# Recurrence scores in compact 32-token blocks, and one shared ring for three work tiles of the feed-forward stages

## The chip, the cores and the metric

The kernel runs on 1 core of one Trainium2 chip. The metric is device time in microseconds (us) of one execution; several executions are timed and their median is given. The engines are named as in the profile: PE (TensorE, matmuls) with PEld (its weight loads), DVE (VectorE), ACT (ScalarE), POOL (GpSimd), and SP, which here only issues DMAs.

## The reference, cut to what matters

One encoder layer on 256 tokens of 2048 features: SwiGLU feed-forward, a mixing stage with two gated recurrences, cross-attention on 256 memory tokens, a second SwiGLU feed-forward, and RMS norms between them, all in float32. The two parts that the change touches are these.

```python
def swiglu(h, w_up, w_down):                     # twice: d_ff is 5632
    gate, up = jnp.split(h @ w_up, 2, axis=-1)
    return (jax.nn.silu(gate) * up) @ w_down

# HGRN2 recurrence, 8 heads of 128 keys and 128 values, in its chunked form
b = jnp.cumsum(gc, axis=2)                       # gc: log of the forget gate
rel = b[:, :, :, None, :] - b[:, :, None, :, :]
decay = jnp.where(tri[None, None, :, :, None], jnp.exp(jnp.minimum(rel, 0.0)), 0.0)
scores = jnp.einsum('bhtk,bhsk,bhtsk->bhts', qc, kc, decay)
o_intra = jnp.einsum('bhts,bhsv->bhtv', scores, vc)
```

So a score of token t against an earlier token s is a product over 128 keys, each damped by the forget gates between s and t.

## The kernel before, in words

**Operands.** Float32 products are made from split operands: a weight tile `raw` (128x2048) is copied by ACT to a rounded high part `h` (line 120), and DVE subtracts it to leave the low part `l` (line 121). Each product then runs as high by high, high by low and low by high matmuls.

**Order of the work.** `plan` (line 127) lists every weight tile in the order of use. `weights()` (line 165) keeps two tiles ahead: before the matmuls of an entry are written down, the tiles of the next entry are loaded and split. The framework orders each engine's queue from this program order and from its own estimate of the times, and places tiles in the buffers of their pools; the engines execute their queues in order. `raw`, `h` and `l` have 3 buffers each.

**Feed-forward (lines 465 to 568).** The up-projection goes in 11 groups of 512 hidden columns. A group is 8 entries; some are "fast" (7 products in place of 8, at the price of sums of weights formed first), the others "mixed" or "plain". From the fourth group (g = 3) on, the fast entries come in the pairs 1 and 3, 4 and 2, 5 and 7, with a mixed entry between pairs; the second and third group (g = 1, 2) have four fast entries, of which 3 and 5 follow each other. Between groups stand 2 or 4 "down" entries. A fast entry uses, besides `raw`, `h` and `l`, two more tiles of 128x2048:

- `td` (line 211): sums of weights, written by DVE in three steps (lines 213, 214, 215), read by the split into `th` and `tl`;
- `tl` (line 219): the low parts of those sums, written by DVE in two halves (line 121) and read by the last matmuls of the entry (line 452).

A third tile, `ev` (line 525), collects a group's results at its end (lines 533 to 546); PE transposes it (line 489) some entries later, in `turn`. Each of the three has a pool of its own with one buffer.

**Recurrence (`hgrn`, lines 749 to 840).** It runs once for heads 0 to 3 and once for heads 4 to 7 (hf = 0, 1), as a generator that is advanced between the weight tiles of other products: `pump(2)` (line 670) after each unit takes two steps, or fewer where a step yields True. What it issues on an engine is queued behind the last matmul of the product. The 256 tokens are two groups (g) of 128. The scores S of 4 heads and 2 groups, 8 squares of 128 by 128, are built in levels: first the diagonal (lines 757 to 764), then for n = 1, 2, 4, ..., 64 the scores between neighbouring runs of n tokens, with q and k damped between levels (line 800).

- Diagonal: per group, 4 matmuls of 128 by 128 (line 760); DVE multiplies the bank by the identity into S (line 762).
- n below 32: 8 matmuls (line 787), each of a whole group's 128 key tokens against the 64 query tokens of that group that stand in odd runs. DVE multiplies the 128x512 bank by a 0/1 mask into a tile `part` (line 790) and adds that into strided columns of S (line 795). Most of what these matmuls compute is masked away, as only runs that are neighbours count.
- n = 32 and 64: small matmuls that compute only the wanted rectangles (line 777), with 32 or 64 stationary columns. For n = 32 the results go to the bank partitions 0 to 31 and 64 to 95, for n = 64 to 0 to 63. ACT copies them into S (line 780).

After the levels one more block (line 809) gives the scores across the two groups, and lines 819 and 820 apply S to the values.

In the profile a float32 matmul of this part shows as two instructions, each with a weight load of its own.

Of the kernel before, what the change touches and what calls it, by code (L numbers as in the profile page):

```python
# [8 lines left out]
F32 = mybir.dt.float32  # L9
# [4 lines left out]
P = 128  # L14
# [15 lines left out]
for _name, _n in [  # L30
    ("ffn1_norm", 16), ("mix_norm", 16), ("xattn_norm", 16), ("mem_norm", 16),
    ("ffn2_norm", 16), ("hgrn_norm", 8), ("lb0", 8), ("lb1", 8), ("lam", 8), ("conv_w", 32),
    ("conv_b", 8), ("ba", 8), ("bx", 8),
    ("ident", P), ("masks", 64 * 5),
]:
    VEC[_name] = (_at, _n)
    _at += _n
# [24 lines left out]
def block_kernel(ctx: ExitStack, tc: tile.TileContext, xT, xin, memT, vec, gfin, bgate, lruw, wu1, wd1, win, wv,  # L62
# [30 lines left out]
    def bank(name="acc"):  # L93
        return psum.tile([P, 512], F32, name=name, tag="acc")
# [100 lines left out]
    def prepare(src, kind, cuts=1):  # L195

        if kind == "added":
            raw, l = begun.pop(0)
            h = hp.tile([P, 2048], F32R, name="h", tag="h")
            done["high"] = act.activation(h, raw, ACT.Copy).ins  # L200
            return h, l
        raw = rawp.tile([P, 2048], F32, name="raw", tag="raw")
        n = 2048 // cuts
        if kind == "plain":
            h, l = split_tiles()
            for a in range(0, 2048, n):
                sp.dma_start(raw[:, a:a + n], src[:, a:a + n])
                split(h[:, a:a + n], l[:, a:a + n], raw[:, a:a + n])
            return h, l
        sp.dma_start(raw, src)  # L210
        td = scoped["td"].tile([P, 2048], F32, name="td", tag="td")
        two = [v[:, a:a + 1024].rearrange("p (i n) -> p i n", i=2) for v, a in ((td, 0), (raw, 512))]
        dve.tensor_tensor(out=two[0], in0=raw[:, None, :512].broadcast_to([P, 2, 512]), in1=two[1], op=ALU.subtract)  # L213
        dve.tensor_tensor(out=td[:, 1024:1536], in0=raw[:, 1024:1536], in1=td[:, :512], op=ALU.subtract)
        dve.tensor_tensor(out=td[:, 1536:], in0=raw[:, 1536:], in1=td[:, 1024:1536], op=ALU.subtract)
        h, l = split_tiles()
        split(h[:, 512:], l[:, 512:], raw[:, 512:])
        th = hp.tile([P, 2048], F32R, name="h", tag="h")
        tl = scoped["tl"].tile([P, 2048], F32R, name="tl", tag="tl")
        for a in (0, 1024):  # L220
            split(th[:, a:a + 1024], tl[:, a:a + 1024], td[:, a:a + 1024])
        return (h, l), (th, tl)
# [114 lines left out]
            return r  # L337


    FFN_POOLS = dict(td=1, tl=1, ev=1, hd=1)  # L340

    class TokenSquares:

# [121 lines left out]
    def ffn(name, pairs, sq, then, begin=(), sums=(), rstds=()):  # L465
# [39 lines left out]
        for at, e in enumerate(order):  # L505
# [3 lines left out]
            if kind != "down":  # L509
                g, p = e[1:]  # L510
                fast = kind == "fast"
                products = []
                for i, (a, b, n) in enumerate(PRODUCTS[kind]):
                    u = uses[g, n]
                    if u[0] == (p, i):
                        accs[n] = bank()
                    own, less = pairs[p]
                    products.append((accs[n], part(own, a, P) if a >= 0 else part(less, -1 - a, P), part(w[b // 4] if fast else w, b % 4, 512),
                                     u[0] == (p, i), u[-1] == (p, i)))
                three(products)  # L520
                last = at + 1 == len(order) or order[at + 1][1] != g or following == "down"
                ends = kind != "plain" and uses[g, 0][-1][0] == p
                if ends or last:
                    if ends or kind == "plain":
                        ev = scoped["ev"].tile([P, 2048], F32, name="ev", tag="ev")
                        e0, e1, e2, e3 = (ev[:, i * 512:(i + 1) * 512] for i in range(4))
                        if rstds:
                            rstd = rstds[0]
                        if rstd is None:
                            with tc.issue_after(done["high"]):  # L530
                                rstd = sq.rstd_tokens()
                if ends:
                    act.activation(e0, accs[0], ACT.Copy)
                    dve.tensor_tensor(out=e1, in0=accs[5], in1=e0, op=ALU.add)
                    dve.tensor_tensor(out=e2, in0=accs[4], in1=e1, op=ALU.add)
                if last:
                    if kind == "plain":
                        activate(e0, accs[0], accs[1], 0)
                        activate(e3, accs[3], accs[2], 1)
                    else:  # L540
                        for o, n, x in ((e0, 1, e0), (e1, 3, e1), (e1, 2, e1)):
                            dve.tensor_tensor(out=o, in0=accs[n], in1=x, op=ALU.add)
                        activate(e0, e0, e1, 0)
                        for o, n, x in ((e3, 6, e2), (e2, 3, e2)):
                            dve.tensor_tensor(out=o, in0=accs[n], in1=x, op=ALU.add)
                        activate(e3, e3, e2, 1)
                    late.append((4 if g else 2, lambda g=g, hid=(e0, e3): turn(g, hid)))
            else:
                first, n, c, block = e[1:]
                if block == first:  # L550
                    accs["down"] = [bank(), bank()]
                for t in range(2):
                    products = []
                    for k in range(4):
                        a = hids[2 * block + k // 2][:, k % 2 * 512:][:, :512]
                        products.append((accs["down"][t], (a[:, t * P:][:, :P], a[:, T + t * P:][:, :P]),
                                         part(w, k, 512), block == first and k == 0, block == first + n - 1 and k == 3))
                    three(products)
                    if block == first + n - 1:
                        o = xt[c][:, t * 512:(t + 1) * 512]  # L560
                        done["residual"] = dve.scalar_tensor_tensor(out=o, in0=accs["down"][t], scalar=0.5, in1=o,
                                                                    op0=ALU.mult, op1=ALU.add).ins
                        if block == NG - 1:
                            then(c, t)
# [184 lines left out]
    def hgrn(hf):  # L749
# [4 lines left out]
        S = scoped["scores"].tile([P, 3 * 512], F32, name="S", tag="S")  # L754
        Sv = S.rearrange("p (g h t) -> p g h t", g=3, h=4)
        qv, kv = heads(q), heads(kk)
        for g in range(2):
            acc = bank()
            for h in range(4):
                pe.matmul(acc[:, h * P:(h + 1) * P], kv[:, h, g * P:(g + 1) * P], qv[:, h, g * P:(g + 1) * P],  # L760
                          start=True, stop=True)
            dve.tensor_tensor(out=Sv[:, g], in0=acc.rearrange("p (h t) -> p h t", h=4),
                              in1=ident[:, None, :].broadcast_to([P, 4, P]), op=ALU.mult)
            yield
        dve.tensor_tensor(out=q, in0=q, in1=f, op=ALU.mult)
        yield True
        tots = slot(name="tots")
# [1 line left out]
        for li, n in enumerate(LEVELS):  # L769
            acc = bank()  # L770
            if n >= 32:
# [8 lines left out]
                    act.activation(S[a:a + n, :1024].rearrange("p (i t) -> p i t", t=P)[:, :, a + n:a + 2 * n],  # L780
                                   acc[a:a + n, :8 * n].rearrange("p (i n) -> p i n", n=n), ACT.Copy)
                yield
            for g in range(2 if n < 32 else 0):
                for h in range(4):
                    i = g * 4 + h
                    r = qv[:, h, g * P:(g + 1) * P].rearrange("p (j two n) -> p j two n", two=2, n=n)[:, :, 1]
                    pe.matmul(acc[:, i * 64:(i + 1) * 64], kv[:, h, g * P:(g + 1) * P], r, start=True, stop=True)  # L787
            if n < 32:
                part = scoped["tmp2"].tile([P, 512], F32, name="part", tag="part")
                dve.tensor_tensor(out=part.rearrange("p (i t) -> p i t", i=8),  # L790
                                  in0=acc.rearrange("p (i t) -> p i t", i=8),
                                  in1=col("masks", li * 64, 64)[:, None, :].broadcast_to([P, 8, 64]), op=ALU.mult)
                yield
                to = S[:, :1024].rearrange("p (i two n) -> p i two n", two=2, n=n)[:, :, 1]
                dve.tensor_tensor(out=to, in0=to, in1=part.rearrange("p (i n) -> p i n", n=n), op=ALU.add)
                yield
            pairs = tot.rearrange("p (j two) -> p j two", two=2)
            for t, side_of, by in ((q, 1, 0), (kk, 0, 1)):
                o = t.rearrange("p (j two n) -> p j two n", two=2, n=n)[:, :, side_of]
# [291 lines left out]
def _layout(inputs):  # L1091
# [43 lines left out]
    put("bx", vector(a["lru_bx"][0]))  # L1135
    put("lam", vector(a["lru_lambda"][0]))
    put("ident", np.eye(P, dtype=np.float32))
    s, t = np.arange(P)[:, None], np.arange(64)[None, :]
    put("masks", np.concatenate([(s // n == 2 * (t // n)) for n in LEVELS[:5]], axis=1).astype(np.float32))

    w = a["w_in"][0]
    win = columns(np.concatenate([w[:, :2048], w[:, 3072:6144]], axis=1))
# [38 lines left out]
```

## Time and profile before

| What | Value |
|---|---|
| Median of 3 runs | 2468.04 us (2466.79 to 2468.06) |
| Span of the profiled execution | 2467.3 us, 0.7 us below the median of the runs; the profile gives no other time for that execution |
| Instructions | 29103 |
| Mean granted PE clock | 0.998 |
| HBM read, written | 472.17 MB, 2.10 MB |

The profile's page gives busy time per engine; other views give groups of instructions by line, the waits by who released them, the busy time in stretches, and the chain of work that ended last, followed back from the last instruction. In the chain a row is a start, a length, and the line with a count of instructions. Times are us unless marked ns. A matmul's listed duration is longer than its distance to the next, because matmuls overlap; the cost of a run of matmuls is read from the chain.

### The profile page before, as it was taken

The numbers are of one execution on the slowest core, as the hardware profiler recorded it, in microseconds if no ns is written. First come the engines' busy times: TensorE is split into PE (matmuls) and PEld (weight loads), VectorE is DVE, ScalarE is ACT, GpSimd is POOL, SyncE is SP. The second block draws the span as 40 slices with busy tenths as digits, with TensorE's granted clock in tenths as the row PEclk, the third lists the DMA queues.
The fourth block names the chain that finished last, engine by engine and source line by source line (L and its number), as shares of the span: only waits on it lengthen the run. The fifth ranks groups of instructions, "written<-read, shape, count | busy, mean of one in ns | idle before, by whom it ended". The sixth has DMA issues, their size and how long they took to land.

```text
span 2467.3 us, 29103 instructions
## 1 busy us (share of the span) xinstructions
PE 2447.8 (99%) x11674; PEld 2045.6 (83%) x11674; DVE 1900.8 (77%) x2018; ACT 1389.5 (56%) x1386; POOL 26.3 (1%) x34
## 2 busy tenths in 40 slices
PE   8999999999999999999999999999999999999998
PEld 7787888888888888888888888888888878888887
DVE  6999999999865757666665676556679989999995
ACT  7556666666564444458434554555555666666664
POOL 0000000000000000000000000000000000000000
PEclk9999999999999999999999999999999999999999
DMA  7557777777655554554655555554555677777774
GB/s 278 192 197 235 231 238 237 238 237 239 226 186 188 171 171 161 173 187 175 224 173 190 202 205 188 171 172 153 186 194 182 221 237 240 238 234 234 235 236 153
DMA packets 75015, 507.61 MB, mean 206 GB/s; under 512 B 8320, under 2 KB 8576, under 8 KB 15232
## 3 DMA queue, kind: packets, MB, share of 16 engines
q1 hardware_dynamic: 69840, 473.17, 55.5%
q0 software_dynamic: 4320, 31.46, 6.4%
q8 instruction: 91, 1.49, 0.2%
q10 hardware_dynamic: 720, 1.13, 0.1%
q14 instruction: 44, 0.36, 0.0%
HBM read 472.17 MB, written 2.10 MB: 192 GB/s over the span
## 4 chain that ended last, share of the span: by engine, by line
PE 95%; ACT 2%; DVE 2%; DMA 1%; issue 0%; SPq 0%; ACTq 0%; DVEq 0%
PE acc L452 17%; PE acc L449 17%; PE acc L450 17%; PE acc L231 11%; PE acc L252 8%; PE acc L253 8%; PE acc L255 8%; PE acc L235 5%; DMA raw<-wu 1%; ACT h L120 1%; PE acc L489 1%; PE acc L787 1%; PE acc L389 1%; DVE l L121 0%; PE acc L1041 0%
## 5 line engine op out<-in xcount | busy, mean ns | idle before, releaser
L121 DVE TENSOR_TENSOR l<-raw,h 128x2048 fp32r<-128x2048 f32 (+2 forms) x422 | 878.6, 2085 | 338.1 <-ACT h L120 334.3
L120 ACT ACTIVATE h<-raw 128x2048 fp32r<-128x2048 f32 (+2 forms) x422 | 738.3, 1752 | 549.7 <-PE acc L253 228.7
L449 PE MATMUL acc<-h,xh 128*128 128x512 f32 x1280 | 501.3, 392 | 8.9 <-ACT h L120 8.9
L450 PE MATMUL acc<-h,xl 128*128 128x512 f32 x1280 | 498.0, 390 | 0.0
L120 ACT ACTIVATE h<-td 128x1024 fp32r<-128x1024 f32 x224 | 235.9, 1055 | 259.6 <-DVE td L213 127.8
L121 DVE TENSOR_TENSOR tl<-td,h 128x1024 fp32r<-128x1024 f32 x224 | 273.1, 1221 | 73.2 <-ACT h L120 45.2
L252 PE MATMUL acc<-h,ops 128*128 128x512 f32 x832 | 326.9, 393 | 0.0
L253 PE MATMUL acc<-h,ops 128*128 128x512 f32 x832 | 324.4, 390 | 0.0
L449 PEld LDWEIGHTS acc<-h,xh 128*128 128x128 f32 x1280 | 240.8, 188 | 64.9 <-ACT h L120 14.2
L450 PEld LDWEIGHTS acc<-h,xl 128*128 128x128 f32 x1280 | 240.9, 188 | 49.3
L231 PE MATMUL acc<-ops,h 128*128 128x512 f32 x1152 | 277.8, 393 | 0.3
L449 PE MATMUL acc<-h,hidop 128*128 128x512 f32 x704 | 275.8, 392 | 0.0
L450 PE MATMUL acc<-h,hidop 128*128 128x512 f32 x704 | 274.4, 390 | 0.0
L231 PEld LDWEIGHTS acc<-ops,h 128*128 128x128 f32 x1152 | 211.9, 188 | 42.6 <-DVE ops L292 0.9
L452 PE MATMUL acc<-l,xh 128*128 128x512 f32 x832 | 218.0, 389 | 0.0
L255 PE MATMUL acc<-l,ops 128*128 128x512 f32 x832 | 205.8, 389 | 0.0
L452 PE MATMUL acc<-l,hidop 128*128 128x512 f32 x704 | 188.4, 389 | 0.0
L255 PEld LDWEIGHTS acc<-l,ops 128*128 128x128 f32 x832 | 156.2, 188 | 32.4
L452 PEld LDWEIGHTS acc<-l,xh 128*128 128x128 f32 x832 | 156.1, 188 | 32.4
L252 PEld LDWEIGHTS acc<-h,ops 128*128 128x128 f32 x832 | 156.3, 188 | 32.2
L253 PEld LDWEIGHTS acc<-h,ops 128*128 128x128 f32 x832 | 156.3, 188 | 31.5
L452 PEld LDWEIGHTS acc<-l,hidop 128*128 128x128 f32 x704 | 132.2, 188 | 27.7
(220 smaller groups left out, 2379.8 us busy)
## 6 DMA issues: line engine op xcount, KB each, us to landing
raw<-wu SPq DMA_DIRECT2D x172, 1024.0 KB, 5.1
raw<-wd SPq DMA_DIRECT2D x88, 1024.0 KB, 4.9
raw<-win SPq DMA_DIRECT2D x40, 1024.0 KB, 4.8
raw<-wg SPq DMA_DIRECT2D x32, 1024.0 KB, 4.8
l<-raw POOLq DMA_DIRECT2D x30, 1024.0 KB, 10.8
raw<-wab SPq DMA_DIRECT2D x16, 1024.0 KB, 4.8
raw<-wout SPq DMA_DIRECT2D x16, 1024.0 KB, 4.8
raw<-wq SPq DMA_DIRECT2D x16, 1024.0 KB, 4.8
```

The source lines that it names most:

```text
L120: done["high"] = act.activation(h, raw, ACT.Copy).ins
L121: dve.tensor_tensor(out=l, in0=raw, in1=h.bitcast(F32), op=ALU.subtract)
L231: pe.matmul(acc, h[:, k * P:(k + 1) * P], xs[k], start=k == 0, stop=False)
L235: done["product"] = pe.matmul(acc[:, :T], l[:, k * P:(k + 1) * P], xs[k][:, :T], start=False, stop=k == KT - 1).ins
L252: pe.matmul(accs[t], x[:, t * P:][:, :P], h[j], start=first and j == 0, stop=False)
L253: pe.matmul(accs[t], x[:, T + t * P:][:, :P], h[j], start=False, stop=False)
L255: done["product"] = pe.matmul(accs[t], x[:, t * P:][:, :P], l[j], start=False, stop=last and j == 3).ins
L389: pe.transpose(accs[m // 2][:, m % 2 * T + t * P:][:, :P], tile[:, t * 512 + m * P:][:, :P], ident)
L449: pe.matmul(acc, ah, bh, start=start, stop=False)
L450: pe.matmul(acc, al, bh, start=False, stop=False)
L452: pe.matmul(acc, ah, bl, start=False, stop=stop)
L489: pe.transpose(acc[:, z * T + t * P:][:, :P], hid[t][:, (2 * y + z) * P:][:, :P], ident)
```

## The change

**Recurrence.** The diagonal and the levels n = 1 to 16 are computed in blocks of 32 tokens: 8 squares of 4 blocks, each block its own matmul of 32 stationary columns, whose result goes to bank partitions b to b + 31 for b = 0, 32, 64, 96 in turn. For the diagonal the moving operand has 32 columns, for a level the 16 query tokens in odd runs of that block. The masks shrink to 32 and 16 columns. The scores within blocks are gathered in a compact tile `near` of 128x256, which lies, with two `part` tiles of 128x128, in the third of S that was unused until the end. After n = 16, four ACT copies place the blocks of `near` in S; before, POOL fills the first 1024 columns of S with zeros. The mask product and the sum of a level are now one step of the generator, and the diagonal is one step in place of two.

**Feed-forward.** `td`, `tl` and `ev` are drawn from one pool, `wide`, with three buffers. All three tiles have the same size, so the space is the same.

```diff
-    ("ident", P), ("masks", 64 * 5),
+    ("ident", P), ("eye", 32), ("masks", 16 * 5),
...
-        td = scoped["td"].tile([P, 2048], F32, name="td", tag="td")
+        td = scoped["wide"].tile([P, 2048], F32, name="td", tag="wide")
...
-        tl = scoped["tl"].tile([P, 2048], F32R, name="tl", tag="tl")
+        tl = scoped["wide"].tile([P, 2048], F32R, name="tl", tag="wide")
...
-    FFN_POOLS = dict(td=1, tl=1, ev=1, hd=1)
+    FFN_POOLS = dict(wide=3, hd=1)
...
-                        ev = scoped["ev"].tile([P, 2048], F32, name="ev", tag="ev")
+                        ev = scoped["wide"].tile([P, 2048], F32, name="ev", tag="wide")
...
-        for g in range(2):
-            acc = bank()
-            for h in range(4):
-                pe.matmul(acc[:, h * P:(h + 1) * P], kv[:, h, g * P:(g + 1) * P], qv[:, h, g * P:(g + 1) * P],
-                          start=True, stop=True)
-            dve.tensor_tensor(out=Sv[:, g], in0=acc.rearrange("p (h t) -> p h t", h=4),
-                              in1=ident[:, None, :].broadcast_to([P, 4, P]), op=ALU.mult)
-            yield
+        near = S[:, 1024:1280]
+        nv = near.rearrange("p (i t) -> p i t", i=8)
+
+        def blocks(acc, n, pick):
+            for i in range(8):
+                g, h = divmod(i, 4)
+                for b in range(0, P, 32):
+                    s = slice(g * P + b, g * P + b + 32)
+                    pe.matmul(acc[b:b + 32, i * n:(i + 1) * n], kv[:, h, s], pick(qv[:, h, s]), start=True, stop=True)
+
+        acc = bank()
+        blocks(acc, 32, lambda t: t)
+        dve.tensor_tensor(out=nv, in0=acc[:, :256].rearrange("p (i t) -> p i t", i=8),
+                          in1=col("eye", 0, 32)[:, None, :].broadcast_to([P, 8, 32]), op=ALU.mult)
+        nc.gpsimd.memset(S[:, :1024], 0.0)
+        yield
...
-            for g in range(2 if n < 32 else 0):
-                for h in range(4):
-                    i = g * 4 + h
-                    r = qv[:, h, g * P:(g + 1) * P].rearrange("p (j two n) -> p j two n", two=2, n=n)[:, :, 1]
-                    pe.matmul(acc[:, i * 64:(i + 1) * 64], kv[:, h, g * P:(g + 1) * P], r, start=True, stop=True)
             if n < 32:
-                part = scoped["tmp2"].tile([P, 512], F32, name="part", tag="part")
+                blocks(acc, 16, lambda t: t.rearrange("p (j two n) -> p j two n", two=2, n=n)[:, :, 1])
+                part = S[:, 1280 + li % 2 * P:][:, :P]
                 dve.tensor_tensor(out=part.rearrange("p (i t) -> p i t", i=8),
-                                  in0=acc.rearrange("p (i t) -> p i t", i=8),
-                                  in1=col("masks", li * 64, 64)[:, None, :].broadcast_to([P, 8, 64]), op=ALU.mult)
-                yield
-                to = S[:, :1024].rearrange("p (i two n) -> p i two n", two=2, n=n)[:, :, 1]
+                                  in0=acc[:, :128].rearrange("p (i t) -> p i t", i=8),
+                                  in1=col("masks", li * 16, 16)[:, None, :].broadcast_to([P, 8, 16]), op=ALU.mult)
+                to = near.rearrange("p (i two n) -> p i two n", two=2, n=n)[:, :, 1]
                 dve.tensor_tensor(out=to, in0=to, in1=part.rearrange("p (i n) -> p i n", n=n), op=ALU.add)
                 yield
+                if n == 16:
+                    for b in range(0, P, 32):
+                        act.activation(S[b:b + 32, :1024].rearrange("p (i t) -> p i t", t=P)[:, :, b:b + 32],
+                                       nv[b:b + 32], ACT.Copy)
```

More of the change, by code (lines that the diff above doesn't have):

```diff
@@ L1137, in _layout @@
     put("ident", np.eye(P, dtype=np.float32))
-    s, t = np.arange(P)[:, None], np.arange(64)[None, :]
-    put("masks", np.concatenate([(s // n == 2 * (t // n)) for n in LEVELS[:5]], axis=1).astype(np.float32))
+    s, t = np.arange(P)[:, None], np.arange(32)[None, :]
+    put("eye", (s % 32 == t[:, :32]).astype(np.float32))
+    put("masks", np.concatenate([(s % 32 // n == 2 * (t[:, :16] // n)) for n in LEVELS[:5]], axis=1).astype(np.float32))
     w = a["w_in"][0]
```

## The prediction, on record before the result

> **What bounds the kernel now.** First the page, for the engines, then the busy time in stretches, for where the busiest one rests.
>
> ```profile
> span 2467.3 us, 29103 instructions
> PE 2447.8 (99%) x11674; PEld 2045.6 (83%) x11674; DVE 1900.8 (77%) x2018; ACT 1389.5 (56%) x1386; POOL 26.3 (1%) x34
> ```
>
> ```profile
> 225.00:250.00 25.00, 23.47 (x103) 18.88 (x102) 21.36 (x22) 14.70 (x12) 1.72 (x2) 1.00 0.83 215
> 250.00:700.00 450.00, 450.00 (x2014) 370.76 (x2012) 402.67 (x410) 278.00 (x231) 10.41 (x12) 1.00 0.74 234
> 700.00:1800.00 1100.00, 1099.73 (x5670) 937.75 (x5669) 698.00 (x805) 562.20 (x654) 0.00 (x0) 1.00 0.53 182
> 1975.00:2000.00 25.00, 23.43 (x103) 18.87 (x102) 20.38 (x19) 16.05 (x13) 0.86 (x1) 1.00 0.90 252
> ```
>
> The columns are the stretch, its length, then the busy time of PE, PEld, DVE, ACT and POOL, the clock, the DMA share and GB/s. PE is busy all the time from 250 to 700 and, but for 0.27, from 700 to 1800, where the recurrence runs; of the 19.5 that it rests in all, 1.5 and 1.6 lie at two spots in the feed-forwards and nearly all else at the start and the end. So in the recurrence only PE's own work counts. DVE is busy there for 698 of 1100: what it saves is worth nothing by itself. In the feed-forward (250 to 700) DVE is busy 403 of 450, so a wait on DVE can reach PE. The waits, PE's and then those of PEld and DVE:
>
> ```profile
> PE acc L449 <- ACT h L120: 8.9, 7, 2.7
> ```
>
> ```profile
> PEld acc L452 <- DVE tl L121: 6.7, 18, 0.8
> ```
>
> ```profile
> DVE tl L121 <- ACT h L120: 45.2, 42, 2.9
> DVE tl L121 <- PE acc L452: 25.3, 31, 3.4
> ```
>
> PE's own waits for split weights are 8.9 in all. But weight loads wait 6.7 for `tl`, 18 times, and DVE waits 25.3 for PE's last use of the single `tl`: that is the wait that a ring can remove.
>
> **The recurrence on PE.** The chain of waits, from 808 to 960, gives what each run of matmuls costs, and the groups by shape give the counts.
>
> ```profile
> 815.78 1.79 PE acc L760 x16
> 817.57 3.67 PE acc L231 x16
> ...
> 823.15 3.65 PE acc L231 x16
> ...
> 828.72 1.74 PE acc L787 x16
> 830.46 3.73 PE acc L231 x16
> ...
> 892.93 0.63 PE acc L777 x32
> 893.56 3.86 PE acc L231 x16
> ...
> 904.89 1.08 PE acc L777 x16
> ```
>
> ```profile
> L787 PE MATMUL acc<-silu,k 128*128 128x64 f32 x160 | 19.0, 271 | 0.0
> L760 PE MATMUL acc<-silu,k 128*128 128x128 f32 x32 | 3.9, 275 | 0.0
> L777 PE MATMUL acc<-silu,k 128*32 128x32 f32 x64 | 1.4, 197 | 0.0
> ```
>
> Removed: L787 is 160 instructions, ten runs of 16 (5 levels, 2 halves of heads). A run takes 1.74, and the 16 full matmuls behind it 3.73 in place of the 3.65 that they take behind other full ones: 1.74 + 0.08 = 1.82. L760 is 32, two runs: 1.79 + 0.02 = 1.81. Moving 64 or 128 columns costs nearly the same (1.74 against 1.79), so the run is set by its 16 loads of 128 stationary columns, and the masked part is cheap to leave in only if the loads stay. Twelve runs: 21.8.
>
> Added: twelve runs of 32 matmuls, 64 instructions, of 32 stationary columns. The nearest row is L777 with 32 columns, which does just this for n = 32 at two bank positions: 32 instructions in 0.63, and 3.86 - 3.65 = 0.21 on the full matmuls behind it. That is 19.7 ns an instruction if nothing in the run is fixed: 64 x 19.7 ns = 1.26, with the 0.21 makes 1.47 a run. If the last matmul's 197 ns is a fixed tail, the rest is 0.43 for 32, or 13.5 ns each: 0.87 + 0.20 + 0.21 = 1.27. I take 1.35, nearer the middle, since part of that tail lies under the next matmul. Saved: 1.82 - 1.35 = 0.47 ten times and 0.46 twice, **5.6 us** (4.2 to 6.6 by the two ends). PE has no rest there, so all of it comes off the time.
>
> The moving operand of a level has 16 columns instead of 32; I count no gain for that, as the old runs show loads to be the limit.
>
> **The recurrence on the others.** On DVE (groups by shape):
>
> ```profile
> L790 DVE TENSOR_TENSOR part<-acc,vt 128x512 f32<-128x512 f32 x10 | 6.8, 681 | 0.0
> L795 DVE TENSOR_TENSOR S<-S,part 128x512 f32<-128x512 f32 x10 | 6.8, 684 | 0.0
> L762 DVE TENSOR_TENSOR S<-acc,vt 128x512 f32<-128x512 f32 x4 | 2.7, 682 | 0.0
> L266 DVE TENSOR_TENSOR sum<-acc,lo 128x256 f32<-128x256 f32 x72 | 29.8, 417 | 0.0
> L432 DVE TENSOR_TENSOR xs<-xg 128x128 f32<-128x128 f32 x40 | 9.8, 284 | 0.0
> ```
>
> ```profile
> L780 ACT ACTIVATE S<-acc 32x256 f32<-32x256 f32 x4 | 1.5, 375 | 0.8 <-PE acc L777 0.8
> ```
>
> Ten masks and ten sums shrink from 128x512 to 128x128 (13.6 to 20 x 0.284 = 5.7), four diagonal products become two of 128x256 (2.7 to 0.8): 9.8 less on DVE, worth 0 beside PE. ACT gets eight copies of 32x256 by 0.375 = 3.0; ACT is busy 562 of 1100 there, and the copies stand ahead of a split that is worked two tiles ahead, so 0. POOL gets two memsets of 128x1024, which no row shows; POOL has 0.00 busy from 700 to 1800, nothing is queued behind them, and their result is first needed by the copies after n = 16, some five levels (65 us at 13 a level) on. So 0; without that cover each would add its own length once in each half. The copies' wait on DVE's last sum is one pump older than they are. A level takes two pumps before and after (its damping of k falls in the second both times), the diagonal one less, so both halves end one unit earlier; PE never waits there, so 0. No DMA moves but the constants' one transfer, which shrinks.
>
> **The ring.** In the steady feed-forward a stall reaches PE once a group; the chain, DVE in order of time, and the loads, at one such place:
>
> ```profile
> 331.34 1.13 PE acc L452 x5
> ...
> 332.93 0.71 PE acc L452 x2
> ```
>
> ```profile
> 328.27 1.22 DVE L121 TENSOR_TENSOR tl<-td,h 128x1024 fp32r<-128x1024 f32 x1 [0.55 <-PE acc L452]
> 329.42 2.28 DVE L121 TENSOR_TENSOR l<-raw,h 128x2048 fp32r<-128x2048 f32 x1
> 331.62 1.22 DVE L121 TENSOR_TENSOR tl<-td,h 128x1024 fp32r<-128x1024 f32 x1
> ```
>
> ```profile
> 332.89 0.30 PEld L452 LDWEIGHTS acc<-tl,xh 128*128 128x128 f32 x2 [0.39 <-DVE tl L121]
> ```
>
> DVE waits 0.55 for PE to leave `tl`, the two halves of the new `tl` come late, and PE loses 0.71 - 2 x 0.226 = 0.26 where the load shows 0.39. Scaled to all 6.7 of such waits, at most 6.7 x 0.26 / 0.39 = 4.5. With three buffers in turn, a `tl` takes the place of the `td` before it, long read, so this wait goes. What is late next is the high half from ACT (the 45.2 of the same view), which the change leaves. So I count half, **2.2 us** (0 to 4.5). The two rests of 1.5 and 1.6 and the start wait for ACT's copies; I count nothing.
>
> Three buffers add two waits: a `td` now waits for PE to have left the `tl` two fast entries back, and near a group's end for the transposes of `ev`. Such a `td` stands at the head of DVE's queue, with the next `l` and `tl` behind it, and PE waits for those. DVE and PE at a group's turn:
>
> ```profile
> 355.16 1.22 DVE L213 TENSOR_TENSOR td<-raw 128x1024 f32<-128x1024 f32 x1
> ```
>
> ```profile
> 349.39 1.03 PE L489 MATMUL acc<-vt,ev 128*128 128x128 f32 x8
> ```
>
> The second `td` of a group starts at 355.16 and would take the place of `ev`, which PE left at 350.4: 4.8 to spare. The `tl` two entries back has at least another entry between: 21 matmuls by 0.226 = 4.7. Both waits are over before `td` is due: 0.
>
> **Sum.** 2467.3 - 5.6 - 2.2 = 2459.5; the runs' median stands 0.7 above this execution, so **2460.2**, say 2460.
>
> **Rivals.** All in terms of the runs' median.
>
> (a) *All four bank positions run at once.* The 32-column row alternates between two positions; if the rate is per position, four double it: the 0.87 of a run becomes 0.43, the run 0.43 + 0.41 = 0.84, and twelve save 11.8. Then 2468.0 - 11.8 - 2.2 = 2454. For it: 64 columns at a single position (1.08 for 16) cost 67 ns an instruction, over three times the 19.7 at two. Against: nothing shows four.
>
> (b) *No overlap between neighbouring positions.* The old row skips a strip (0 and 64); 0 and 32 may share something. Then 32 columns cost half of the 67 ns, 34: 64 x 34 = 2.16, + 0.21 = 2.37 a run, 0.55 more than now, 6.6 in all. 2468.0 + 6.6 - 2.2 = 2472.4. The Trainium skill, "TensorE: Matmul & The Clock Gate", "The mechanism" in Part 3, says that a weight load runs beside a matmul only where the row groups differ, and all these use all rows. By that rule this rival is the forecast; the trace, with 19.7 ns on the same rows, doesn't bear it out.
>
> (c) *A least distance between matmul starts.* A run breaks even at (1.82 - 0.21) / 64 = 25.2 ns. If starts of such short matmuls can't come closer on average, PE saves nothing: 2468.0 - 2.2 = 2465.8. Against it: 19.7 in the row above, over 32 instructions. The same page, "Wait — 56ns, not 53.3ns?" in Part 1, says that starts never come closer than about 25 ns; by that figure, an estimate, a run would be 1.81 and the saving 0. The trace differs.
>
> (d) *The ring stalls DVE; slower.* In each pair of fast entries the second `td` comes out of turn, waits at the head of DVE's queue for PE, and delays `l` and `tl`. A group is 270 matmuls (6 x 21, 2 x 24 and 4 downs of 24) by 0.226, 61 us; DVE rests 450 - 403 = 47 in 450, 6.4 a group, so it decides once the waits of a group pass about that; a stall is priced by the one above, 0.26. Eight groups of three pairs and two of one are 26 pairs, in two feed-forwards 52: if each cost one stall, 13.5. 2468.0 - 5.6 + 13.5 = 2476. For it: the queue's order is fixed ahead, on estimated times. Against: the 4.8 and 4.7 to spare.
>
> That the ring changes nothing is the forecast's upper end: 2468.0 - 5.6 = 2462.4.
>
> **Chances.** Forecast 0.45 (2457 to 2463), (a) 0.15, (b) 0.10, (c) 0.15, (d) 0.15. A measurement of this kernel can tell about 0.2%, 5 us, from no change: faster means below 2463, slower above 2473. Faster: forecast and (a), 0.60. Same: (c) and half of (b), 0.20. Slower: (d) and the other half of (b), 0.20. The range leaves out (d) and reaches over (a) and (b): 2453 to 2473.
>
> **What would show it.** The new runs in the chain: 64 instructions in about 1.14, then 3.86 (right); 0.63 says (a), 1.6 says (c), over 2 says (b). PE busy from 700 to 1800 unbroken, and this stretch's work shorter by 5.6. The wait of `tl` on PE's L452 gone from DVE's list, and the loads' 6.7 about halved. New waits of `td` on PE or on the transposes, with PE waiting for `tl` or `h` in each group, say (d). Wrong beyond all this would be a rest of PE in the recurrence, for the mask product or for POOL.

## The result, and the profile after

The changed kernel takes **2456.35 us** (median of 4 runs, 2454.64 to 2456.61) against 2468.05 (4 runs, 2466.79 to 2469.03): a ratio of 0.9952 [0.9938, 0.9966]. It is faster by 11.7, or 0.5%, where 7.8 was forecast. The page of the profile after:

```profile
span 2454.8 us, 30191 instructions
PE 2434.6 (99%) x12250; PEld 2036.9 (83%) x12250; DVE 1894.1 (77%) x2016; ACT 1391.2 (57%) x1398; POOL 28.3 (1%) x36
```

The same stretches as before, with the same columns:

```profile
225.00:250.00 25.00, 25.00 (x114) 20.74 (x113) 22.38 (x24) 18.52 (x16) 1.73 (x2) 1.00 0.89 241
250.00:700.00 450.00, 450.00 (x2023) 372.95 (x2022) 405.18 (x410) 272.38 (x233) 11.39 (x13) 1.00 0.70 232
700.00:1800.00 1100.00, 1099.74 (x6297) 933.46 (x6296) 693.90 (x807) 577.93 (x670) 0.95 (x1) 1.00 0.52 184
```

PE is still the bound: busy throughout the recurrence, and the page counts 576 more matmuls in a span that is 12.5 shorter. The rest of 1.5 that stood between 225 and 250 is gone; two longer ones stand at other places, as shown below.

To see where the time went, I cut the span at two lines that only the middle part has, the first start of L231 and the last of L255. Their rows, first of before, then of after (count, ns min/median/max, first to last start):

```profile
L231 PE MATMUL acc<-ops,h x1152: 387/389/586, 714.2 to 1559.0; 128*128 128x512 f32 x192
L255 PE MATMUL acc<-l,ops x832: 388/389/582, 764.1 to 1762.4; 128*128 128x512 f32 x167
```

```profile
L231 PE MATMUL acc<-ops,h x1152: 387/389/579, 712.0 to 1545.9; 128*128 128x512 f32 x192
L255 PE MATMUL acc<-l,ops x832: 387/389/582, 762.0 to 1749.4; 128*128 128x512 f32 x167
```

The middle part took 1762.4 - 714.2 = 1048.2 and takes 1037.4: **10.8 less**, nearly the whole gain. What follows it took 2467.3 - 1762.4 = 704.9 and takes 705.4. The first stretch is 2.2 shorter (714.2, 712.0), but two kernels below with the feed-forward of after have 714.1 and 714.7 there, so 2.2 in one profile is no effect.

The chain of waits of after, in the same place as before, shows the new runs:

```profile
813.63 0.69 PE acc L765 x50
814.32 3.86 PE acc L231 x16
...
820.09 0.67 PE acc L765 x52
```

A run has 64 instructions (L765 has 768 in the twelve runs; the chain names only some of them) and takes 0.67 to 0.69, not the 1.14 that would have meant "right"; 0.63 was the sign of rival (a). The 3.86 behind it is as forecast. So a run costs 0.67 + 0.21 = 0.88 in place of 1.82, and twelve save 11.3, against 10.8 measured. The other new work that has a new shape, from the groups by shape:

```profile
L802 ACT ACTIVATE S<-S 32x256 f32<-32x256 f32 x8 | 3.3, 413 | 3.5 <-DVE S L798 3.4
L771 POOL MEMSET S<- 128x1024 f32 x2 | 1.9, 956 | 307.8 <-DVE plain L266 285.9 <-DVE tl L121 21.8
```

None of it reaches PE: 1099.74 of 1100 leaves no room.

**The feed-forward.** The waits of before for the high half, of which the prediction showed only PE's own, and then the waits of after (total, times, longest):

```profile
PEld acc L449 <- ACT h L120: 14.2, 16, 3.1
```

```profile
PEld acc L449 <- ACT h L120: 9.7, 8, 3.4
PE acc L449 <- ACT h L120: 7.0, 4, 3.0
PEld acc L452 <- DVE tl L121: 4.1, 3, 3.5
PE acc L452 <- DVE tl L121: 3.0, 1, 3.0
DVE td L213 <- DMA raw<-wu: 7.2, 5, 3.4
DVE td L213 <- PE acc L452: 2.0, 2, 1.0
DVE tl L121 <- PE acc L452: 0.4, 1, 0.4
```

The 18 small waits for `tl` are now 3, but one of these is 3.5 long: the steady stalls are gone and something larger has come. DVE's first `td` step now waits 7.2 for loads, a wait that before does not list. Two rests of 3.0 are new. The chain at the first and the load ahead of the second, then the windows at both, all of after:

```profile
178.49 10.33 DMA raw<-wu
...
188.92 2.44 ACT h L120 x2
...
194.74 0.43 PE acc L450
195.17 1.54 PE acc L452 x5
196.71 0.23 PE acc L449
...
197.63 1.13 PE acc L452 x5
...
1915.19 10.65 DMA raw<-wu
```

```profile
188.00:192.00 4.00, 0.98 (x5) 0.51 (x4) 2.79 (x2) 2.43 (x2) 0.00 (x0) 1.00 0.72 264
192.00:194.00 2.00, 2.00 (x7) 1.62 (x6) 1.97 (x4) 0.57 (x1) 0.00 (x0) 0.62 1.00 422
194.00:196.00 2.00, 2.00 (x6) 1.52 (x6) 1.80 (x2) 1.54 (x2) 0.00 (x0) 0.53 0.53 143
196.00:198.00 2.00, 2.00 (x11) 1.62 (x10) 1.25 (x2) 0.33 (x1) 0.00 (x0) 1.00 0.81 319
...
1930.00:1932.00 2.00, 2.00 (x7) 1.52 (x6) 2.00 (x3) 0.79 (x1) 0.00 (x0) 0.50 0.01 4
```

And how long the loads of L210 take in after:

```profile
DMA to landing us min/median/max: 4.6/4.9/10.7
```

Read it from the back. PE rests 4.00 - 0.98 = 3.0 for a high half, whose copy stands in ACT's queue behind one that waits for a weight load; that load takes 10.33, where the median is 4.9, because the accumulating transfer of a mixed entry (`l` from `raw`, issued at 176.48) moves beside it, as e7 shows below; and the load starts at 178.49, when the last `td` step has read its buffer.

The long load alone does not make the rest. In e1, the kernel below without the ring, the same load in the order of loads starts at 178.9 and is long too, but PE does not rest there:

```profile
DMA to landing us min/median/max: 9.2/9.2/9.2
```

What differs is the order of ACT's queue. First its rows in e1, then in after:

```profile
187.21 1.04 ACT L120 ACTIVATE h<-td 128x1024 fp32r<-128x1024 f32 x1
188.21 1.50 ACT L120 ACTIVATE h<-raw 128x1536 fp32r<-128x1536 f32 x1
```

```profile
188.92 1.48 ACT L120 ACTIVATE h<-raw 128x1536 fp32r<-128x1536 f32 x1 [3.14 <-DMA raw<-wu]
190.31 1.04 ACT L120 ACTIVATE h<-td 128x1024 fp32r<-128x1024 f32 x1
```

The `td` row is the second half of the entry before the load's, the `raw` row the copy of the loaded tile. With the ring the second half stands behind the copy that waits for the load, and PE waits for the second half; in e1 it is ready at 188.25, before PE comes to it.

Then comes a second loss: after the rest the granted clock is 0.62 and 0.53 in the two windows of 2 us, and six matmuls lie 0.43 apart instead of 0.23 and five of L452 take 1.54 instead of 1.13, some 1.6 in all. In the profile of before the clock is 1.00 behind both of its rests.

The second rest of after, also of 3.0, begins at 1925, with a load of 10.65 ahead of it and a clock of 0.50 behind it. Here PE waits for the second half of a `tl`, and the queue is DVE's: the half stands behind the first `td` step on the late load.

```profile
1925.94 1.23 DVE L213 TENSOR_TENSOR td<-raw 128x1024 f32<-128x1024 f32 x1 [3.39 <-DMA raw<-wu]
1927.09 1.22 DVE L121 TENSOR_TENSOR tl<-td,h 128x1024 fp32r<-128x1024 f32 x1
```

In e1 the same load starts at 1915.0 and takes 10.2, but there the half of `tl` is made at 1924.04 and the `td` step follows at 1925.31.

### The profile page after: what moved, and what is told of

The parts are those of the page before. It is cut to its first block, busy times and chain, and to the rows that moved or that the text cites. A ratio compares the mean times of both kernels' runs of the same rounds, so it can differ in the third digit from the quotient of the medians.

```text
span 2454.8 us, 30191 instructions
## 1 busy us (share of the span) xinstructions
PE 2434.6 (99%) x12250; PEld 2036.9 (83%) x12250; DVE 1894.1 (77%) x2016; ACT 1391.2 (57%) x1398; POOL 28.3 (1%) x36
## 3 DMA queue, kind: packets, MB, share of 16 engines
q10 hardware_dynamic: 720, 1.13, 0.1%
## 4 chain that ended last, share of the span: by engine, by line
PE 95%; DVE 2%; ACT 1%; DMA 1%; issue 0%; SPq 0%; ACTq 0%; DVEq 0%
PE acc L449 17%; PE acc L450 17%; PE acc L452 17%; PE acc L231 11%; PE acc L252 8%; PE acc L253 8%; PE acc L255 8%; PE acc L235 5%; DMA raw<-wu 1%; PE acc L489 1%; ACT h L120 1%; DVE l L121 1%; PE acc L389 1%; PE acc L765 0%; PE acc L1048 0%; PE acc L1003 0%
## 5 line engine op out<-in xcount | busy, mean ns | idle before, releaser
L120 ACT ACTIVATE h<-td 128x1024 fp32r<-128x1024 f32 x224 | 229.6, 1055 | 178.4 <-PE acc L450 131.0
L121 DVE TENSOR_TENSOR tl<-td,h 128x1024 fp32r<-128x1024 f32 x224 | 267.4, 1221 | 33.6 <-ACT h L120 31.0
L231 PE MATMUL acc<-ops,h 128*128 128x512 f32 x1152 | 278.0, 393 | 0.3
L231 PEld LDWEIGHTS acc<-ops,h 128*128 128x128 f32 x1152 | 211.9, 188 | 42.9 <-DVE ops L292 0.9
L452 PE MATMUL acc<-l,xh 128*128 128x512 f32 x832 | 218.9, 390 | 0.0
L255 PE MATMUL acc<-l,ops 128*128 128x512 f32 x832 | 206.1, 390 | 0.0
L452 PE MATMUL acc<-l,hidop 128*128 128x512 f32 x704 | 188.3, 389 | 0.0
L452 PEld LDWEIGHTS acc<-l,xh 128*128 128x128 f32 x832 | 156.5, 188 | 32.6
L255 PEld LDWEIGHTS acc<-l,ops 128*128 128x128 f32 x832 | 156.2, 188 | 32.4
L452 PEld LDWEIGHTS acc<-l,hidop 128*128 128x128 f32 x704 | 132.2, 188 | 27.5
```

The costliest lines, as they stand in the source:

```text
L121: dve.tensor_tensor(out=l, in0=raw, in1=h.bitcast(F32), op=ALU.subtract)
L231: pe.matmul(acc, h[:, k * P:(k + 1) * P], xs[k], start=k == 0, stop=False)
L255: done["product"] = pe.matmul(accs[t], x[:, t * P:][:, :P], l[j], start=False, stop=last and j == 3).ins
L452: pe.matmul(acc, ah, bl, start=False, stop=stop)
```

## The experiments

All ratios are to runs of the kernel before on the same chip; e7 to e10 ran on another chip than e1 to e4, and before has 2467.24 there against 2468.10, so medians across the two groups differ by up to 0.9 for that alone. The edits are against the kernel after. One table holds what the cuts at L231 and L255 give for every kernel; the columns are us to the first L231, from there to the last L255, and from there to the span's end.

| Kernel | median | ratio | to L231 | middle | behind |
|---|---|---|---|---|---|
| before | 2468.05 | | 714.2 | 1048.2 | 704.9 |
| after | 2456.35 | 0.9952 | 712.0 | 1037.4 | 705.4 |
| e1, blocks only | 2456.05 | 0.9954 | 712.0 | 1037.2 | 704.8 |
| e2, ring only | 2464.97 | 0.9989 | 711.9 | 1048.3 | 702.4 |
| e3, one position | 2473.07 (1 run) | | 714.7 | 1051.2 | 705.4 |
| e4, two positions | 2462.97 (1 run) | | 714.1 | 1041.6 | 705.5 |
| e7, accumulate later | 2451.01 | 0.9933 | 710.1 | 1037.4 | 702.1 |
| e8, four `raw` | 2446.99 | 0.9917 | 707.3 | 1038.3 | 700.3 |
| e9, four `raw`, no ring | 2455.29 | 0.9949 | 711.2 | 1038.3 | 703.9 |
| e10, 22 slots | 2457.82 | 0.9962 | 712.2 | 1038.3 | 704.9 |

**Blocks alone.** `td`, `tl` and `ev` go back to pools of their own.

```diff
-        td = scoped["wide"].tile([P, 2048], F32, name="td", tag="wide")
+        td = scoped["td"].tile([P, 2048], F32, name="td", tag="td")
...
-    FFN_POOLS = dict(wide=3, hd=1)
+    FFN_POOLS = dict(td=1, tl=1, ev=1, hd=1)
```

> The recurrence in blocks of 32 tokens, with the three feed-forward tiles back in pools of their own. Theory (the blocks give nearly all of the gain, through PE's runs of matmuls alone): the stretch between the feed-forwards is 10.9 us shorter than before, as in the changed kernel (1037.6 against 1048.5), both feed-forwards are as before, with the two rests of about 1.6 us at 237 and about 1973; time 2468.05 - 10.9 = 2457.1. Rival (the ring gives part of the gain): over 2458.5, with the middle shorter by less than 9.

Measured: 0.9954 [0.9942, 0.9967], the middle as in after. The blocks alone give the whole gain; on top of them the ring gives nothing (2456.35 against 2456.05). The waits for `tl` are those of before, and near 188 PE does not rest; its two rests of 1.5 begin at 236 and 1972, as in before:

```profile
PEld acc L452 <- DVE tl L121: 6.7, 18, 0.8
```

```profile
184.00:200.00 16.00, 16.00 (x72) 12.86 (x71) 14.26 (x15) 9.94 (x9) 0.00 (x0) 1.00 0.74 268
```

**Ring alone.** The recurrence goes back to the code of before; `td`, `tl` and `ev` share the ring.

```diff
-        acc = bank()
-        blocks(acc, 32, lambda t: t)
...
+        for g in range(2):
+            acc = bank()
+            for h in range(4):
+                pe.matmul(acc[:, h * P:(h + 1) * P], kv[:, h, g * P:(g + 1) * P], qv[:, h, g * P:(g + 1) * P],
+                          start=True, stop=True)
```

> The ring of three tiles alone, the recurrence as before. Theory (the ring takes away the small stalls on tl in each group, and pays it back in one longer rest per feed-forward): first feed-forward about 2 us shorter, second about 0.7 us longer, the middle 1048.5 as before; PE rests of about 3 us near 188 and near 1938 with the clock below 0.7 just after; time 2466 to 2468. Rival 1 (the ring is pure gain, and the long rests come with the smaller constants or the blocks): no rest over 2 us between 100 and 700, time 2463 to 2465. Rival 2 (the ring stalls DVE in each pair of fast entries): over 2470.

Measured: 0.9989 [0.998, 0.9998], 3.1 less than before and 1.0 under the expected range, with the middle unchanged; its runs spread over 3.4. The small waits are gone and the long load near 178 is there again:

```profile
178.51 10.22 DMA raw<-wu
```

```profile
PEld acc L452 <- DVE tl L121: 2.8, 3, 2.0
```

By its time alone this would be rival 1, but rival 1 has no rest over 2, and there is one of 3.4 near 188. So that rest comes with the ring, and so does the order of the queues: ACT's copy of `raw` at 188.84 stands ahead of that of `td` at 190.23, and DVE's `td` step at 1935.16 ahead of `tl` at 1936.30. The second rest, near 1936, is only 1.6, with a clock of 1.00 behind it, and the stretch behind the middle is 2.5 shorter. That is some 2.6 less lost than in after, which fits a ring that is worth 3.1 here and nothing on top of the blocks.

**One bank position for eight blocks in a row.** The same matmuls in another order.

```diff
-            for i in range(8):
-                g, h = divmod(i, 4)
-                for b in range(0, P, 32):
+            for b in range(0, P, 32):
+                for i in range(8):
+                    g, h = divmod(i, 4)
```

> The changed kernel, with the 32 matmuls of a run ordered so that eight in a row go to the same 32 bank partitions. Theory (the rate is limited per bank position, and positions run beside each other): a run of 64 instructions takes about 2.1 us in place of 0.67 (34 ns each, half of the 67 ns that 64 columns take at one position), twelve runs add 17 us, time about 2473. Rival (a 32-column load simply costs 10 ns wherever its result goes): 0.67 us a run, time 2456.

Its chain:

```profile
816.25 1.84 PE acc L765 x64
```

28.7 ns an instruction where 34 was expected, and a middle 13.8 longer than in after, against 12 x (1.84 - 0.67) = 14.0. That the time meets the expected 2473 is in part chance: another 2.7 lies ahead of the middle. The matmuls are the same and only their order differs, so the order sets the rate. I put it down to the bank position; with it the square changes too, at each matmul here, at every second in e4 and every fourth in after, and no run separates the two.

**Two positions in turn.** The blocks alternate between 0 and 32, then between 64 and 96.

```diff
-            for i in range(8):
-                g, h = divmod(i, 4)
-                for b in range(0, P, 32):
+            for i, b in [(i, a + 32 * z) for a in (0, 64) for i in range(8) for z in range(2)]:
+                    g, h = divmod(i, 4)
```

> The changed kernel, with the matmuls of a run ordered so that 16 alternate between bank partitions 0 and 32, then 16 between 64 and 96. Theory (rate per position): about 1.1 us a run, as the rows for n = 32 gave for two positions, twelve runs add about 5 us, time about 2461. Rival (no limit per position): 0.67 us and 2456. Second rival (neighbouring strips share something that 0 and 64 do not): 2 us a run, 2472.

```profile
815.62 1.04 PE acc L764 x62
```

16.3 ns an instruction, and a middle 4.2 longer than in after (12 x 0.37 = 4.4). Neighbouring positions overlap as well as 0 and 64 did in the old row for n = 32. One, two and four positions in turn give 1.84, 1.04 and 0.67.

**The accumulating transfer later.** The mixed entries of the fourth group do without it, so that none is near 188.

```diff
-            kind = "fast" if e[0] == "fast" else "added" if e[0] == "mixed" and e[1:] > (3, 0) else "plain"
+            kind = "fast" if e[0] == "fast" else "added" if e[0] == "mixed" and e[1:] > (3, 6) else "plain"
```

> The changed kernel, where the first entry whose low part is made by a DMA accumulate comes one group-end later: entry 6 of the fourth group is split by ACT and DVE as a plain one. Theory (the long rest is a weight load that runs beside the accumulate DMA and takes 10.3 us in place of 4.8): no rest over 1 us near 188 and 1925, that load lands in 5 to 6 us; if nothing else follows, each feed-forward is 3 to 5 us shorter, time 2447 to 2450; the same meeting may come back one group later, as the kernel before has it at 237 with 1.6 us, then about 2453. Rival (the load is late because DVE frees its buffer late; the accumulate has no part): the rest stays at 3 us, time 2456.

Measured: 0.9933 [0.9919, 0.9946], 5.3 less than after (4.7 by the ratios), between the two times that were expected. The rests at 188 and 1925 are gone, and the meeting comes again a group later: a load in the chain, then the windows.

```profile
224.20 9.56 DMA raw<-wu
```

```profile
234.00:237.00 3.00, 1.18 (x6) 0.67 (x5) 2.70 (x2) 2.29 (x2) 0.00 (x0) 1.00 0.76 265
237.00:239.00 2.00, 2.00 (x8) 1.58 (x7) 1.97 (x4) 0.45 (x1) 0.00 (x0) 0.67 0.99 414
239.00:241.00 2.00, 2.00 (x7) 1.52 (x6) 0.60 (x1) 2.00 (x2) 0.23 (x1) 0.50 0.77 270
```

The long load goes where the first accumulating transfer goes. This rest is 1.8, and the clock still falls behind it.

**A fourth buffer for `raw`.** Two token slots are given up for the space.

```diff
-    rawp = pool("raw", 3)
+    rawp = pool("raw", 4)
...
-    slots = pool("slots", 24)
+    slots = pool("slots", 22)
```

> The changed kernel with four buffers for the loaded weight tiles in place of three (and 22 slots in place of 24, to make room). Theory (the load needs its buffer earlier; beside the accumulate it takes 10 us, but started one entry earlier it is in time): the rests near 188 and 1925 fall below 1 us, time 2448 to 2452. Rival (the accumulate only meets another load): a rest of 1.5 to 3 us stays somewhere in the fourth or fifth group, time 2454 to 2457.

Measured: **2446.99**, 0.9917 [0.9904, 0.9931], the fastest of all and under the expected range. Its windows and its waits of `td` for loads:

```profile
100.00:225.00 125.00, 125.00 (x565) 103.67 (x564) 122.76 (x130) 72.56 (x62) 1.87 (x2) 1.00 0.59 210
225.00:700.00 475.00, 475.00 (x2136) 393.52 (x2135) 425.34 (x431) 292.30 (x251) 12.25 (x14) 1.00 0.71 234
...
1790.00:2430.00 640.00, 640.00 (x2867) 530.19 (x2867) 577.60 (x550) 383.02 (x317) 13.04 (x15) 1.00 0.66 222
```

```profile
PEld acc L449 <- ACT h L120: 5.8, 5, 3.2
...
DVE td L213 <- DMA raw<-wu: 1.6, 2, 1.1
...
PEld acc L452 <- DVE tl L121: 0.3, 1, 0.3
```

PE rests nowhere in these stretches. ACT's queue has the order of after (the copy of `raw` at 185.22, that of `td` at 186.62), but the load in question starts at 172.8 and takes 4.8. Other loads still take up to 10.5 beside an accumulating transfer; they now start early enough.

**Four `raw` without the ring**, and as a control **after with 22 slots and three `raw`**. Their edits are combinations of those above.

> The recurrence in blocks with separate td, tl and ev, four buffers for loaded tiles and 22 slots. Theory (the rests of 1.6 us near 235 and 1972 go with the earlier load, but the small stalls on tl of each group, 0.24 us, stay without the ring): 2452 to 2454, so 2 to 4 us above the same with the ring. Rival (the ring has no part in the steady groups): equal to the run with the ring and four buffers.

> The changed kernel with 22 slots in place of 24 and nothing else: the control for the runs with four buffers. Expected by both theories: as the changed kernel within its spread, 2455 to 2457, as slots are spare in the feed-forwards; if 22 slots cost something it is in the middle stretch.

Measured: 0.9949 [0.9936, 0.9963] and 0.9962 [0.9948, 0.9976]. Giving up the slots gains nothing by itself (2457.82, 0.8 over the expected range; the middle is 1038.3 in all three kernels with 22 slots, 0.9 over after), so the fourth buffer is worth 10.8 with the ring. Without it e9 and e1 differ by 0.8 (2455.29 against 2456.05), across two chips and with two slots fewer, which does not tell a gain from none. The ring is worth 0 with three `raw` and **8.3 with four** (2455.29 - 2446.99), where 2 to 4 were expected. The waits of e9:

```profile
PEld acc L449 <- ACT h L120: 8.2, 12, 3.2
PEld acc L452 <- DVE tl L121: 8.2, 22, 0.8
```

## Why the prediction was right, and where it was wrong

**The time** lies in the forecast range, and the direction was right. That it lies within 4 of the forecast is in part luck: the blocks saved 5.7 more than their term, the ring 2.2 less, and the range was wide enough to hold rival (a) as well.

**The bound** held: PE has no rest in the recurrence in either kernel, so what its matmuls save there comes off the time, and what DVE, ACT and POOL gain or get there is worth nothing. The middle part follows PE's runs to within 0.5 in after, e3 and e4.

**The size of the run was wrong.** The step that failed is "I take 1.35": the rate of the nearest row was carried over without its condition. That row alternates between two bank positions, and for two positions the estimate was good: e4 has 1.04 + 0.21 = 1.25 beside the lower bound of 1.27. But the new runs go through four positions, and e3, e4 and after show that the rate goes with them. The cost of a run is 0.88, the saving 11.3 instead of 5.6. That is rival (a), which I gave 0.15 because nothing showed four positions; the row of 67 ns at one position, which I put down in its favour, was worth more than that.

**Rivals (b) and (c) are refuted** by e4 and after: neighbours overlap, and starts lie 10.5 ns apart on average, under the 25.2 ns at which nothing is saved. The Trainium skill, "TensorE: Matmul & The Clock Gate", speaks on both sides here. Its floor of about 25 ns between starts (Part 1, "Wait — 56ns, not 53.3ns?") does not hold for these runs at two or four positions, nor does its rule that a weight load overlaps with matmuls in flight only across row groups (Part 3, "The mechanism"): all of these use all rows, and an instruction with its load takes 28.7 at one position and 10.5 at four. But its table in Part 3, "Measured speedup vs the span model", lists 2.38 times for three column positions, which I did not weigh; the runs give 1.84 / 1.04 = 1.8 for two and 1.84 / 0.67 = 2.7 for four, and are in line with it, though the table's moving operand has 512 columns.

**The ring** was wrong in both its halves, which cancel in after. The forecast of 2.2 was too small for what it removes: DVE's wait for PE to leave `tl` fell from 25.3 to 0.4. Where loads come early (e9 to e8) the ring takes 7.9 from the waits for `tl` and 2.4 from those for the high half; 10.3 x 0.26 / 0.39, by the prediction's own scale, is 6.9, and 8.3 was measured. I had halved the sum because the high half would be late next; it came earlier too. The other half is "The two rests of 1.5 and 1.6 and the start wait for ACT's copies; I count nothing": with the ring these two are gone, and two of 3.0, which take the clock with them, come at other places. The ring changes the order of ACT's and DVE's queues, and a half that PE needs then stands behind the first step on a load that runs beside the accumulating transfer. Both are needed: in e1 the load lands nearly as late (188.1 against 188.8) and the order is another, in e8 the order is that of after and the load early, and neither rests there. In e2 both are present, and in e7 the load is short, as the transfer is elsewhere. Why the queues are ordered as they are was only read from the traces, not tried.

**The waits that the ring adds** were put at 0. DVE's `td` waits for PE 2.0 in all, at two places, and rival (d) with its 52 stalls did not come about. The 7.2 that `td` waits for loads was in neither the sum nor the rivals.

## What to carry to other kernels

A rate taken from a profile holds with its layout: ask how many bank positions the measured row used, and whether the new code uses more. A buffer that removes a wait moves the engines' whole order; look at what now stands behind the first step on a late load, and try a buffer for the loads before judging the first one. On top of the blocks neither the ring nor the fourth load buffer gave a gain that these runs can tell; together they gave 9.1 (2456.05 to 2446.99, and 9.1 by the ratios).

## What the runs showed of the hardware

- Float32 matmuls of 32 stationary and 16 or 32 moving columns cost 28.7 ns an instruction in the order with one bank position at a time (e3), 16.3 with two (e4) and 10.5 with four (after).
- A load of 1 MB beside an accumulating transfer on chip can take twice as long: 10.33 and 10.65 in after, 9.56 in e7, where the median of L210 in after is 4.9. Not every such load does: the one that starts at 175.62 in after, beside the same transfer, takes 5.8.
- Rests of PE of 1.5 and 1.6 left the granted clock at 1.00; rests of 1.8 (e7) and 3.0 (after) were followed by less: in windows of 1 us from 192 to 196, after has 0.73, 0.50, 0.50 and 0.56, and 1.00 behind them. The Trainium skill, "TensorE: Matmul & The Clock Gate", "What's actually happening" in Part 1, has the clock halved after an idle window of about 3.4 us that runs freely; the halving agrees, but here a rest of 1.8 was enough.
